# A Griffin-style decoder layer on one core: down-projection sums rescheduled over fourteen units, and the last half's embedding, squares and stores rearranged

## The chip, the cores and the metric

The kernel runs on one core of a Trainium2 chip. The metric is the device time of one execution in microseconds. TensorE (PE) multiplies matrices, VectorE (DVE), ScalarE (ACT) and GpSimd (POOL) work element by element, SyncE (SP) issues nearly all the transfers (DMA). Each engine runs its instructions in the order in which they stand in the program; an instruction that waits holds up everything behind it on its engine.

## The reference

One layer of a hybrid decoder, 1024 tokens by 1024 features, float32. What matters here comes after the two attention branches:

```
h  += SwiGLU(RMSNorm(h))                   # silu(n W_gate) * (n W_up), then W_down;  D_FF = 2816
h  += sigmoid(h W_g) * RMSNorm(p[i] W_p)   # a gated embedding of the layer
out = RMSNorm(h)
```

## The kernel before, in words

Every float32 product is made of three TensorE passes over operands split in a high and a low part (`split`, lines 130 to 132: a cast on ACT at L131, a subtraction on DVE at L132; `passes`, lines 134 to 139). Activations are held transposed, 128 features by 512 tokens to a tile; 512 tokens are a half.

**Gate and up, 985 to 1432 us.** The two wide products are made with a seven-product (Winograd) scheme. One unit `wino` is a block of 256 columns of one of the two weights: 7 products of 12 matmuls, some 19.4 us of TensorE. Even units u are gate units, odd ones up units; the loop `for n, u in enumerate(rest())` runs 19 units, n = 0 to 18, which are u = 3 to 21. The loop interleaves the products of neighbouring units. A product's weight block is split into a tile `wl` (three buffers) before TensorE may read it: cast on ACT, L132 on DVE. Two sums of weight blocks are made ahead on POOL (L969, L970) as soon as the unit's 1 MB of raw weights has landed, two more later (L986, L988). PSUM accumulators `pP`, `pQ`, `pR` are added to stored copies by DVE (`add`, L979). In an up unit the finished blocks are multiplied with those of the gate unit on POOL (L1034) or DVE (L1036), subtracted from each other on DVE (`sub`, L1027) and stored to `d_g`.

**Down sums.** The down projection uses the same scheme, so sums of blocks of its weight are made ahead, beside gate and up. `down_in(kk)` loads four blocks of 256 KB into half of the tile `spare` (L1113); `down_sums(kk, ...)` makes four sums in place on DVE (L1120, two operands in SBUF, 128x512) and stores each to `d_w` (L1121). There are KK = 11 such sets. Four loads of 512 KB (L1142) then fill `spare` with the first blocks for the down stage.

**Down, 1432 to 1650 us**, reads `d_g` and `d_w` back. **Gated embedding, 1650 us to the end:** three groups, (half 1, all 512 tokens), (half 0, first 256), (half 0, last 256). In each, for f = 0 to 7: load of the embedding tile e (L1231), scaling with gain and reciprocal root (L1232, DVE), 24 matmuls into `pg`, sigmoid (L1238, ACT), e = sg * e (L1239, DVE), h = e + h (L1241, DVE), square (L1245, ACT), and acc += square (L1246, DVE). Then the squares are summed over partitions by `rstd_cols` (matmuls `pm`, L168; `rstd_finish`, L172 on DVE and L173 on POOL), `spread` turns the result into a row broadcast over partitions (L742 on DVE, matmul `bc`, L745), and eight tiles are scaled (L1252, DVE) and stored (L1254, SP).

The program's order is made by a scheduler from its own model of the engines, so an edit in one place can move instructions elsewhere. `tc.issue_after(x)` keeps what stands under it behind instruction x.

Of the kernel before, what the change touches and what calls it, by code (L numbers as in the profile page):

```python
# [10 lines left out]
F32 = mybir.dt.float32  # L11
# [8 lines left out]
P = 128  # L20
# [31 lines left out]
def decoder_layer(ctx: ExitStack, tc: tile.TileContext, x, p, positions, g_mix, w_in, g_q_a, w_q_b,  # L52
# [104 lines left out]
    with ExitStack() as att:  # L157
# [341 lines left out]
        with ExitStack() as ml:  # L499
# [5 lines left out]
            def slot(tag, name, dtype=F32R):  # L505
                return qkp.tile([P, S], dtype, name=name, tag=tag, bufs=2 if tag == "vst" else 3)
# [450 lines left out]
    t1_factors(quarter[0], bc0)  # L957
    acc = out_group(1, 2, 2)

    FIRST = (1, 2, 5, 6, 7, 3, 4)  # L960
    firsts = iter((M, O, B))
    ORDER = (1, 5, 2, 6, 7, 3, 4)

    def wino(raw, order, ctile, ready):
# [11 lines left out]
            nc.scalar.copy(out=s[key], in_=pt)  # L976

        def add(key, pt):
            nc.vector.tensor_tensor(out=s[key], in0=pt, in1=s[key], op=ALU.add)  # L979
            return s[key]  # L980

        for n, i in enumerate(order):
# [141 lines left out]
    DIRECT = {1: (0, 0), 2: (0, 1), 4: (1, 1)}  # L1124
    before = None
    blocks = {}
    for n, u in enumerate(rest()):

        if 2 <= n < KK + 2:
            blocks[n - 2] = down_in(n - 2)  # L1130
        for _ in range(2):
            next(u)
        for _ in before or ():
            pass
        for _ in range(3):
            next(u)
        before = u
        if 3 <= n < KK + 3:
            down_sums(n - 3, blocks.pop(n - 3))
        if n == KK + 4:  # L1140
            for kk in range(0, 8, 2):
                nc.sync.dma_start(out=spare[:, kk:kk + 2, :], in_=wd[0, :, kk:kk + 2, hcol(0)])  # L1142

# [69 lines left out]
    for hf in (1, 0):  # L1213
        bc[hf] = spread(wk.tile([P, HALF], F32, name="diag", tag="rr", bufs=10), r_ple[:, 4 * hf:4 * hf + 4])
        if hf:
            es = wk.tile([P, HALF], F32, name="bcs", tag="bcs")
            nc.scalar.copy(out=es, in_=bc[hf])
            bc[hf] = es
    for hf, c0, n in ((1, 0, 4), (0, 0, 2), (0, 2, 2)):
        c = slice(c0 * P, (c0 + n) * P)  # L1220
        w_ = slice(0, n * P)
        s = slice(hf * HALF + c0 * P, hf * HALF + (c0 + n) * P)
        acc = wk.tile([P, 2, HALF], F32, name="acc", tag="rs", bufs=3)
        for f in range(NK):
            w = wpg[f // 2][:, f % 2]
            if hf == 1:
                raw = wk.tile([P, NK, P], F32, name="raw", tag="ls", bufs=3)
                nc.sync.dma_start(out=raw, in_=w_ple_gate[:, f * P:(f + 1) * P].rearrange("(k p) n -> p k n", p=P))
                split(w[:, 0], w[:, 1], raw)
            e = wk.tile([P, HALF], F32, name="e", tag="rr", bufs=10)[:, w_]  # L1230
            nc.sync.dma_start(out=e, in_=d_e[f * P:(f + 1) * P, s])  # L1231
            nc.vector.scalar_tensor_tensor(out=e, in0=e, scalar=gains[:, 1, f:f + 1], in1=bc[hf][:, c],  # L1232
                                           op0=ALU.mult, op1=ALU.mult)
            pg = ps.tile([P, HALF], F32, name="pg", **big())[:, w_]
            passes(pg, [((w[:, 0, k, :], w[:, 1, k, :]), (hsp[hf, k // 4][:, 0, k % 4, c], hsp[hf, k // 4][:, 1, k % 4, c]))
                        for k in range(NK)])
# [5 lines left out]
            if f == 0:  # L1242
                nc.scalar.activation(out=acc[:, 0, w_], in_=h, func=AF.Square, scale=1.0 / 32.0)
            else:
                nc.scalar.activation(out=sg, in_=h, func=AF.Square, scale=1.0 / 32.0)  # L1245
                nc.vector.tensor_tensor(out=acc[:, 0, w_], in0=acc[:, 0, w_], in1=sg, op=ALU.add)  # L1246
        r = wk.tile([P, 4], F32, name="r", tag="r", bufs=2)
        rstd_cols(acc[:, 0, :], r[:, 0:n], n)
        bo = spread(acc[:, 1, :], r[:, 0:n], n, B)[:, w_]
        for f in range(NK):  # L1250
            o = wk.tile([P, HALF], F32, name="o", tag="rr", bufs=10)[:, w_]
            nc.vector.scalar_tensor_tensor(out=o, in0=hres[:, f, s], scalar=gains[:, 2, f:f + 1], in1=bo,  # L1252
                                           op0=ALU.mult, op1=ALU.mult)
            nc.sync.dma_start(out=out[f * P:(f + 1) * P, s], in_=o)  # L1254
    dn.close()
    mo.close()

# [32 lines left out]
```

## Time and profile before

| | us |
|---|---|
| median of 3 runs (lowest, highest) | 1770.49 (1769.61, 1770.96) |
| the profiled execution | 1764.39 |
| its span, first to last instruction | 1762.7 |
| TensorE busy | 1689.8 (96%) |
| VectorE, ScalarE, GpSimd busy | 1159.9, 893.1, 368.1 |
| mean granted clock of TensorE, share of full | 0.987 |

The profiled execution is one single run, 6.1 us below the median of the others. Busy times of different engines overlap; idle time of an engine that nobody waits for costs nothing. The rows of the profile that matter stand below.

### The profile page before, as it was taken

To read this page: it belongs to the slowest core of one execution; us is meant where nothing else is said; L and a number is where in the kernel's file an instruction comes from. 1 tells how busy PE (TensorE), PEld (TensorE's weight loads), DVE (VectorE), ACT (ScalarE), POOL (GpSimd) and SP (SyncE) were. 2 spreads that over 40 slices of the span, in tenths; PEclk is the share of its full clock that TensorE was granted. 3 is DMA by queue.
4 is the path that set the end of the run, shared out by engine and by line. 5 is a ranking of instruction groups with operands and counts; after the bars stand their busy time and mean duration, and the time that the engine had idled before them with its cause. 6 is when DMAs were issued, how large, how long until landed. Compare 5 with 4: busy or idle time off the path is not lost.

```text
span 1762.7 us, 23332 instructions
## 1 busy us (share of the span) xinstructions
PE 1689.8 (96%) x8148; PEld 1406.3 (80%) x8148; DVE 1159.9 (66%) x2079; ACT 893.1 (51%) x1740; POOL 368.1 (21%) x393
## 2 busy tenths in 40 slices
PE   6999999999999999998999999899999999999995
PEld 5888878888787888886889778688888878888795
DVE  6667788768875877787368865744444545656655
ACT  5265676667775776676135533233333334445411
POOL 2011320000211433331001823344344310000000
PEclk9999999999999999999999899999999999999998
DMA  5211221213414321215763584842233338666422
GB/s 173 55 54 44 71 61 43 78 43 90 126 37 156 103 67 63 76 49 206 266 241 121 179 274 151 274 153 92 94 111 104 108 116 291 195 196 192 145 71 74
DMA packets 169400, 222.15 MB, mean 126 GB/s; under 512 B 23298, under 2 KB 100098, under 8 KB 169282
## 3 DMA queue, kind: packets, MB, share of 16 engines
q1 hardware_dynamic: 163250, 200.74, 35.4%
q0 software_dynamic: 6032, 19.93, 3.2%
q8 instruction: 64, 1.05, 0.3%
q14 instruction: 54, 0.44, 0.1%
HBM read 151.93 MB, written 67.90 MB: 125 GB/s over the span
## 4 chain that ended last, share of the span: by engine, by line
PE 72%; DVE 9%; issue 7%; DMA 7%; ACT 2%; POOL 2%; SPq 0%; POOLq 0%; DVEq 0%; ACTq 0%
PE pt L137 5%; PE pt L138 5%; PE pt L139 5%; PE pd L138 3%; PE pd L137 3%; PE pd L139 3%; PE pP L139 3%; PE pP L137 3%; PE pP L138 3%; DMA spare<-w_ffn_down 2%; PE pQ L137 2%; PE pQ L138 2%; PE pg L137 2%; PE pQ L139 2%; PE pg L139 2%
## 5 line engine op out<-in xcount | busy, mean ns | idle before, releaser
L137 PE MATMUL pt<-nTh,w_h 128*128 128x512 f32 (+1 forms) x480 | 190.8, 398 | 3.5 <-ACT go L355 2.4
L138 PE MATMUL pt<-nTl,w_h 128*128 128x512 f32 (+1 forms) x480 | 188.5, 393 | 0.0
L139 PE MATMUL pt<-nTh,w_l 128*128 128x512 f32 (+1 forms) x480 | 187.6, 392 | 0.0
L132 DVE TENSOR_TENSOR wl<-raw,wl 128x512 fp32r<-128x512 f32 x132 | 98.7, 750 | 97.5 <-ACT wl L131 97.0
L139 PE MATMUL pP<-b,wl 128*128 128x512 f32 x352 | 139.0, 397 | 11.4 <-DVE wl L132 11.4
L131 ACT CAST wl<-raw 128x512 fp32r<-128x512 f32 x132 | 82.0, 622 | 125.2 <-PE pP L139 53.4
L137 PE MATMUL pP<-b,wl 128*128 128x512 f32 x352 | 139.6, 397 | 5.7 <-ACT wl L131 3.5
L138 PE MATMUL pP<-b,wl 128*128 128x512 f32 x352 | 139.4, 396 | 0.0
L137 PEld LDWEIGHTS pt<-nTh,w_h 128*128 128x128 f32 (+1 forms) x480 | 89.7, 187 | 25.7 <-ACT go L355 5.9
L139 PEld LDWEIGHTS pt<-nTh,w_l 128*128 128x128 f32 (+1 forms) x480 | 89.8, 187 | 19.2
L138 PEld LDWEIGHTS pt<-nTl,w_h 128*128 128x128 f32 (+1 forms) x480 | 89.9, 187 | 18.2
L132 DVE TENSOR_TENSOR drs<-drr,drs 128x512 fp32r<-128x512 f32 x74 | 50.9, 690 | 76.3 <-ACT drs L131 76.3
L138 PE MATMUL pd<-drs,dls 128*128 128x512 f32 x296 | 100.7, 390 | 0.1
L139 PE MATMUL pd<-drs,dls 128*128 128x512 f32 x296 | 100.4, 389 | 0.0
L137 PE MATMUL pd<-drs,dls 128*128 128x512 f32 x296 | 99.9, 392 | 0.0
L131 ACT CAST drs<-drr 128x512 fp32r<-128x512 f32 x74 | 45.9, 623 | 103.2 <-PE pd L139 92.6
L139 PEld LDWEIGHTS pP<-b,wl 128*128 128x128 f32 x352 | 67.2, 191 | 29.8 <-DVE wl L132 15.9
L638 POOL TENSOR_SCALAR pw<-pw,st 128x128 f32<-128x128 f32 (+5 forms) x48 | 74.4, 1556 | 63.9 <-PE tp L652 13.9
L137 PEld LDWEIGHTS pP<-b,wl 128*128 128x128 f32 x352 | 67.4, 192 | 20.4 <-ACT wl L131 3.8
L138 PEld LDWEIGHTS pP<-b,wl 128*128 128x128 f32 x352 | 67.4, 191 | 14.2
L445 DVE TENSOR_TENSOR sz<-sz,T 128x512 f32<-128x512 f32 (+2 forms) x96 | 52.2, 550 | 33.8 <-PE T L443 33.0
L356 POOL DMA_DIRECT2D d_gate<-go x32 | 17.7, 554 | 260.2 <-ACT go L355 218.3
(371 smaller groups left out, 4792.6 us busy)
## 6 DMA issues: line engine op xcount, KB each, us to landing
d_g<-t SPq DMA_DIRECT2D x74, 256.0 KB, 2.0
drr<-d_g SPq DMA_DIRECT2D x74, 256.0 KB, 2.9
w_raw<-w_in SPq DMA_DIRECT2D x33, 512.0 KB, 4.4
raw<-w_ffn_gate SPq DMA_DIRECT2D x11, 1024.0 KB, 5.6
raw<-w_ffn_up SPq DMA_DIRECT2D x11, 1024.0 KB, 5.6
spare<-w_ffn_down SPq DMA_DIRECT2D x44, 256.0 KB, 3.8
d_w<-spare SPq DMA_DIRECT2D x44, 256.0 KB, 3.3
drr<-d_w SPq DMA_DIRECT2D x44, 256.0 KB, 2.7
```

The source lines that it names most:

```text
L131: nc.scalar.copy(out=h, in_=src)
L132: eng.tensor_tensor(out=l, in0=src, in1=r32(h), op=ALU.subtract)
L137: nc.tensor.matmul(ps, lhsT=ah, rhs=bh, start=first and i == 0, stop=False, **kw)
L138: nc.tensor.matmul(ps, lhsT=ah, rhs=bl, start=False, stop=False, **kw)
L139: nc.tensor.matmul(ps, lhsT=al, rhs=bh, start=False, stop=last and i == n - 1, **kw)
L356: nc.gpsimd.dma_start(out=dst, in_=go[0:rows, :])
L445: nc.vector.tensor_tensor(out=sz[:, c0:], in0=sz[:, c0:], in1=T[:, c0:], op=ALU.subtract)
L638: nc.gpsimd.tensor_scalar(out=pw[:, 0:nk], in0=pw[:, 0:nk], scalar1=st[:, 6:7], scalar2=None, op0=ALU.mult)
```

## The change

It has two parts. In gate and up, the eleven sets of down sums are spread: set kk is loaded at n = 2 + 5*kk//4 (2, 3, 4, 5, 7, 8, 9, 10, 12, 13, 14; before: 2 to 12) and summed one n later, and its sums are held behind the latest accumulator add of the unit, which is the one on `pP`. The last four loads of `spare` come one n later. In the gated embedding, half 0's embedding is loaded into one tile `en` (16 KB in each partition, four transfers of 512 KB) and scaled once over 512 tokens, in place of sixteen tiles of 256 tokens; the squares of the last f are not added to acc on DVE but summed by more matmuls into `pm`; the outputs are written over `hres`, and go out in four stores of two tiles, two of which ACT's queue issues in the last group.

```
@@ wino @@
         def add(key, pt):
-            nc.vector.tensor_tensor(out=s[key], in0=pt, in1=s[key], op=ALU.add)
+            latest["add"] = nc.vector.tensor_tensor(out=s[key], in0=pt, in1=s[key], op=ALU.add).ins
@@ loop over the units @@
+    when = {2 + 5 * kk // 4: kk for kk in range(KK)}
     for n, u in enumerate(rest()):
-        if 2 <= n < KK + 2:
-            blocks[n - 2] = down_in(n - 2)
+        if n in when:
+            blocks[when[n]] = down_in(when[n])
...
-        if 3 <= n < KK + 3:
-            down_sums(n - 3, blocks.pop(n - 3))
-        if n == KK + 4:
+        if n - 1 in when:
+            with tc.issue_after(latest["add"]):
+                down_sums(when[n - 1], blocks.pop(when[n - 1]))
+        if n == KK + 5:
@@ gated embedding @@
+        if hf == 0 and en is None:
+            en = slot(2, "en", [P, NK, HALF], F32)
+            for f in range(0, NK, 2):
+                nc.sync.dma_start(out=en[:, f:f + 2, :], in_=d_e[f * P:(f + 2) * P, hcol(0)]
+                                  .rearrange("(k p) n -> p k n", p=P))
+            for f in range(NK):
+                nc.vector.scalar_tensor_tensor(out=en[:, f, :], in0=en[:, f, :], scalar=gains[:, 1, f:f + 1], in1=bc[0],
+                                               op0=ALU.mult, op1=ALU.mult)
...
-            e = wk.tile([P, HALF], F32, name="e", tag="rr", bufs=10)[:, w_]
-            nc.sync.dma_start(out=e, in_=d_e[f * P:(f + 1) * P, s])
...
+            else:
+                e = en[:, f, c]
...
-                nc.vector.tensor_tensor(out=acc[:, 0, w_], in0=acc[:, 0, w_], in1=sg, op=ALU.add)
+                if f < NK - 1:
+                    nc.vector.tensor_tensor(out=acc[:, 0, w_], in0=acc[:, 0, w_], in1=sg, op=ALU.add)
-        rstd_cols(acc[:, 0, :], r[:, 0:n], n)
+        pt = ps.tile([P, HALF], F32, name="pm", **M)
+        for sq in (acc[:, 0, :], sg):
+            for i in range(n):
+                nc.tensor.matmul(pt[:, i:i + 1], lhsT=sq[:, i * P:(i + 1) * P], rhs=ones, start=sq is not sg and i == 0,
+                                 stop=sq is sg, skip_group_check=True)
+        rstd_finish(pt, r[:, 0:n], n)
...
-            nc.sync.dma_start(out=out[f * P:(f + 1) * P, s], in_=o)
+            if f % 2:
+                eng = nc.scalar if c0 and f % 4 == 1 else nc.sync
+                eng.dma_start(out=out[(f - 1) * P:(f + 1) * P, s].rearrange("(k p) n -> p k n", p=P),
+                              in_=hres[:, f - 1:f + 1, s])
```

The tile `en` takes the memory of `hs[1, 0]`, the first half of the features of half 1, so its loads wait for TensorE's last read of that. Lines behind the changed ones move by a few numbers: L979 becomes L980, L1027 L1028, L1034 L1035, L1036 L1037, L1120 and L1121 become L1121 and L1122; in the gated embedding L1232 becomes L1235 (half 0) and L1246 (half 1), L1239 L1255, L1241 L1257, L1246 L1263, L168 L1268, L1252 L1273, L1254 L1277.

How the order changes, at three places. The first is VectorE around the sums. In the program of before they stand between the splits (L132) and the adds (L979); this is where units u = 4 and 5 meet, 1100 to 1115 us:

```order
1328 L1120 TENSOR_TENSOR spare<-spare 128x512
1329 L979 TENSOR_TENSOR t<-pQ,t 128x512
1330 L132 TENSOR_TENSOR wl<-raw,wl 128x512 x2
1331 L1120 TENSOR_TENSOR spare<-spare 128x512
1332 L979 TENSOR_TENSOR t<-pR,t 128x512
1333 L132 TENSOR_TENSOR wl<-raw,wl 128x512
1334 L1120 TENSOR_TENSOR spare<-spare 128x512 x3
1335 L132 TENSOR_TENSOR wl<-s_10697,wl 128x512
```

In the changed program the first set stands behind the `pP` add of unit u = 6, and in each of the eleven units that carry one it stands thus:

```order
1325 L980 TENSOR_TENSOR t<-pP,t 128x512
1326 L1121 TENSOR_TENSOR spare<-spare 128x512
1327 L132 TENSOR_TENSOR wl<-raw,wl 128x512
1328 L1121 TENSOR_TENSOR spare<-spare 128x512 x3
1329 L132 TENSOR_TENSOR wl<-raw,wl 128x512
1330 L980 TENSOR_TENSOR t<-pQ,t 128x512
```

The sums have moved from all over the unit to one place behind the `pP` add, with one split between the first and the other three.

The second place is VectorE in the up unit u = 7, from its `pQ` add on, before:

```order
1370 L979 TENSOR_TENSOR t<-pQ,t 128x512
1371 L132 TENSOR_TENSOR wl<-raw,wl 128x512
1372 L1036 TENSOR_TENSOR t<-pP,t 128x512
1373 L1027 TENSOR_TENSOR t<-t 128x512
1374 L132 TENSOR_TENSOR wl<-raw,wl 128x512
1375 L1027 TENSOR_TENSOR t<-t 128x512 x2
1376 L979 TENSOR_TENSOR t<-pR,t 128x512
1377 L132 TENSOR_TENSOR wl<-raw,wl 128x512
```

and in the changed program:

```order
1341 L980 TENSOR_TENSOR t<-pQ,t 128x512
1342 L132 TENSOR_TENSOR wl<-raw,wl 128x512
1343 L1028 TENSOR_TENSOR t<-t 128x512
1344 L1037 TENSOR_TENSOR t<-pP,t 128x512
1345 L1028 TENSOR_TENSOR t<-t 128x512
1346 L132 TENSOR_TENSOR wl<-raw,wl 128x512
1347 L1028 TENSOR_TENSOR t<-t 128x512
1348 L980 TENSOR_TENSOR t<-pR,t 128x512
1349 L1028 TENSOR_TENSOR t<-t 128x512
1350 L132 TENSOR_TENSOR wl<-raw,wl 128x512
```

The first subtraction (now L1028) has moved ahead of the `pP` product, and one more now stands ahead of the last split shown; so it is in u = 7, 9, 11, 13 and 17. On POOL the third L1035 of these units now stands ahead of both sums of the next raw weights (L970, L971), where before it stood between the two.

The third place is the passage from group 1 to group 2 of the gated embedding, VectorE, before:

```order
1713 L1239 TENSOR_TENSOR e<-sg,e 128x512
1714 L1241 TENSOR_TENSOR hres<-e,hres 128x512
1715 L1246 TENSOR_TENSOR acc<-acc,sg 128x512
1716 L172 TENSOR_SCALAR r<-pm 128x4
1717 L742 TENSOR_SCALAR acc<-ident,r 128x128 x4
1718 L1252 SCALAR_TENSOR_TENSOR o<-hres,cols,bc 128x512 x8
1719 L1232 SCALAR_TENSOR_TENSOR e<-e,cols,bc 128x256 x2
```

and in the changed program, where L1255 and L1257 are the last f of group 1:

```order
1716 L1235 SCALAR_TENSOR_TENSOR en<-en,cols,bc 128x512 x2
1717 L1255 TENSOR_TENSOR e<-sg,e 128x512
1718 L1235 SCALAR_TENSOR_TENSOR en<-en,cols,bc 128x512 x2
1719 L1257 TENSOR_TENSOR hres<-e,hres 128x512
1720 L1235 SCALAR_TENSOR_TENSOR en<-en,cols,bc 128x512 x4
1721 L172 TENSOR_SCALAR r<-pm 128x4
1722 L742 TENSOR_SCALAR acc<-ident,r 128x128 x4
1723 L1273 SCALAR_TENSOR_TENSOR hres<-hres,cols,bc 128x512 x8
```

The eight scalings of `en` stand between and around the last product and sum of group 1, and ahead of L172; each waits for its transfer.

## Rows read from the trace of the kernel before

In a row of a timeline: start in us, duration, engine, line, operation, out<-in, count; in square brackets the engine's idle time ahead of it and what ended that.

**Rows 1.** The page, busy time of each engine with its share of the span and its count of instructions.

```profile
PE 1689.8 (96%) x8148; PEld 1406.3 (80%) x8148; DVE 1159.9 (66%) x2079; ACT 893.1 (51%) x1740; POOL 368.1 (21%) x393
```

**Rows 2.** TensorE's waits between 860 and 1460 us: who waited for whom, us in total, times, longest.

```profile
PE pP L139 <- DVE wl L132: 11.4, 10, 4.6
```

**Rows 3.** TensorE's timeline, the instructions that ended a wait in gate and up.

```profile
1008.13 0.50 PE L137 MATMUL pR<-b,wl 128*128 128x512 f32 x1 [0.59 <-DVE spare L979]
1017.12 0.50 PE L139 MATMUL pQ<-b,wl 128*128 128x512 f32 x1 [0.53 <-DVE wl L132]
1026.48 0.50 PE L139 MATMUL pP<-b,wl 128*128 128x512 f32 x1 [0.67 <-DVE wl L132]
1037.17 0.50 PE L137 MATMUL pP<-b,wl 128*128 128x512 f32 x1 [2.22 <-DVE spare L979]
1110.94 0.50 PE L139 MATMUL pP<-b,wl 128*128 128x512 f32 x1 [4.63 <-DVE wl L132]
1134.35 0.50 PE L139 MATMUL pP<-b,wl 128*128 128x512 f32 x1 [2.45 <-DVE wl L132]
1174.92 0.50 PE L139 MATMUL pP<-b,wl 128*128 128x512 f32 x1 [0.52 <-DVE wl L132]
1214.03 0.50 PE L139 MATMUL pP<-b,wl 128*128 128x512 f32 x1 [0.74 <-DVE wl L132]
```

**Rows 4.** The sums' line L1120: for what VectorE sat idle ahead of them, us and times.

```profile
  DMA spare<-w_ffn_down: 24.0, 10
```

**Rows 5.** VectorE's timeline between 1108 and 1134 us.

```profile
1108.99 0.69 DVE L1120 TENSOR_TENSOR spare<-spare 128x512 f32<-128x512 f32 x1 [5.15 <-DMA spare<-w_ffn_down]
1110.20 0.68 DVE L132 TENSOR_TENSOR wl<-raw,wl 128x512 fp32r<-128x512 f32 x1
1126.92 0.69 DVE L1027 TENSOR_TENSOR t<-t 128x512 f32<-128x512 f32 x1 [1.18 <-POOL t L1034]
1133.02 0.68 DVE L1120 TENSOR_TENSOR spare<-spare 128x512 f32<-128x512 f32 x1
```

**Rows 6.** Windows: from:to, length, then busy us and count of PE, its weight loads, DVE, ACT, POOL, the granted clock of TensorE as a share of full, DMA share, GB/s.

```profile
1037.00:1041.00 4.00, 3.83 (x17) 3.14 (x18) 2.01 (x4) 2.52 (x5) 0.00 (x0) 1.00 0.94 290
1111.00:1115.00 4.00, 4.00 (x11) 3.13 (x12) 3.93 (x4) 0.00 (x0) 2.71 (x2) 0.57 0.40 153
1135.00:1139.00 4.00, 4.00 (x12) 3.12 (x11) 2.79 (x3) 0.82 (x2) 1.04 (x1) 0.57 0.86 330
```

**Rows 7.** Timelines of VectorE, then GpSimd, around the end of the up unit u = 7, where the kernel before has no sums.

```profile
1164.24 0.69 DVE L132 TENSOR_TENSOR wl<-raw,wl 128x512 fp32r<-128x512 f32 x1 [2.51 <-ACT wl L131]
1169.97 1.77 DVE L1027 TENSOR_TENSOR t<-t 128x512 f32<-128x512 f32 x1 [0.73 <-POOL t L1034]
...
1167.39 1.29 POOL L969 TENSOR_TENSOR s<-raw 128x512 f32<-128x512 f32 x1 [1.02 <-DMA raw<-w_ffn_gate]
1169.89 1.29 POOL L970 TENSOR_TENSOR raw<-raw 128x512 f32<-128x512 f32 x1
```

**Rows 8.** TensorE's timeline in the last group of the gated embedding.

```profile
1737.95 0.38 PE L137 MATMUL pg<-hs,wpg 128*128 128x256 f32 x1 [1.24 <-ACT sg L1238]
1751.67 0.38 PE L168 MATMUL pm<-cols,acc 128*128 128x1 f32 x1 [7.72 <-DVE acc L1246]
```

**Rows 9.** Timelines of VectorE, then ScalarE, in the same stretch.

```profile
1739.71 0.48 DVE L1232 SCALAR_TENSOR_TENSOR e<-e,cols,bc 128x256 f32<-128x256 f32 x1 [2.54 <-DMA e<-d_e]
1749.14 0.42 DVE L1239 TENSOR_TENSOR e<-sg,e 128x256 f32<-128x256 f32 x1
1749.81 0.42 DVE L1241 TENSOR_TENSOR hres<-e,hres 128x256 f32<-128x256 f32 x1
1750.14 1.48 DVE L1246 TENSOR_TENSOR acc<-acc,sg 128x256 f32<-128x256 f32 x3
1755.56 3.22 DVE L1252 SCALAR_TENSOR_TENSOR o<-hres,cols,bc 128x256 f32<-128x256 f32 x8 [1.31 <-PE bc L745]
...
1738.72 0.38 ACT L1238 ACTIVATE sg<-pg 128x256 f32<-128x256 f32 x1
1750.32 0.42 ACT L1245 ACTIVATE sg<-hres 128x256 f32<-128x256 f32 x1 [0.59 <-DVE hres L1241]
```

**Rows 10.** SyncE's queue at the end (start, time over which it issued, count), then the list of transfers between 1655 and 1765 us: count, KB each, median us from issue to landing.

```profile
1756.07 3.77 SPq L1254 DMA_DIRECT2D out<-o  x8
...
out<-o SPq DMA_DIRECT2D x8, 256.0 KB, 3.1
out<-o SPq DMA_DIRECT2D x16, 128.0 KB, 1.8
```

**Rows 11.** The passage from group 1 to group 2: timelines of TensorE, then VectorE, then two lines of the list of transfers of the whole span.

```profile
1688.20 0.39 PE L137 MATMUL pg<-hs,wpg 128*128 128x512 f32 x1
1700.00 0.95 PE L168 MATMUL pm<-cols,acc 128*128 128x1 f32 x8
...
1690.37 0.74 DVE L1232 SCALAR_TENSOR_TENSOR e<-e,cols,bcs 128x512 f32<-128x512 f32 x1
1694.47 0.69 DVE L1239 TENSOR_TENSOR e<-sg,e 128x512 f32<-128x512 f32 x1 [2.57 <-ACT sg L1238]
...
raw<-w_ple_gate SPq DMA_DIRECT2D x8, 512.0 KB, 4.6
hres<-d_h SPq DMA_DIRECT2D x4, 1024.0 KB, 10.9
```

More of the change, by code (lines that the diff above doesn't have):

```diff
@@ L958, in decoder_layer @@
     acc = out_group(1, 2, 2)
+    latest = {}
     FIRST = (1, 2, 5, 6, 7, 3, 4)
@@ L1218, in decoder_layer @@
             bc[hf] = es
+    en = None
     for hf, c0, n in ((1, 0, 4), (0, 0, 2), (0, 2, 2)):
@@ L1229, in decoder_layer @@
                 split(w[:, 0], w[:, 1], raw)
-            e = wk.tile([P, HALF], F32, name="e", tag="rr", bufs=10)[:, w_]
-            nc.sync.dma_start(out=e, in_=d_e[f * P:(f + 1) * P, s])
-            nc.vector.scalar_tensor_tensor(out=e, in0=e, scalar=gains[:, 1, f:f + 1], in1=bc[hf][:, c],
-                                           op0=ALU.mult, op1=ALU.mult)
+            if hf:
+                e = wk.tile([P, HALF], F32, name="e", tag="rr", bufs=10)
+                nc.sync.dma_start(out=e, in_=d_e[f * P:(f + 1) * P, s])
+                nc.vector.scalar_tensor_tensor(out=e, in0=e, scalar=gains[:, 1, f:f + 1], in1=bc[hf],
+                                               op0=ALU.mult, op1=ALU.mult)
+            else:
+                e = en[:, f, c]
             pg = ps.tile([P, HALF], F32, name="pg", **big())[:, w_]
@@ L1245, in decoder_layer @@
                 nc.scalar.activation(out=sg, in_=h, func=AF.Square, scale=1.0 / 32.0)
-                nc.vector.tensor_tensor(out=acc[:, 0, w_], in0=acc[:, 0, w_], in1=sg, op=ALU.add)
+                if f < NK - 1:
+                    nc.vector.tensor_tensor(out=acc[:, 0, w_], in0=acc[:, 0, w_], in1=sg, op=ALU.add)
         r = wk.tile([P, 4], F32, name="r", tag="r", bufs=2)
-        rstd_cols(acc[:, 0, :], r[:, 0:n], n)
+        pt = ps.tile([P, HALF], F32, name="pm", **M)
[4 more added lines that the diff above has]
+        rstd_finish(pt, r[:, 0:n], n)
         bo = spread(acc[:, 1, :], r[:, 0:n], n, B)[:, w_]
         for f in range(NK):
-            o = wk.tile([P, HALF], F32, name="o", tag="rr", bufs=10)[:, w_]
-            nc.vector.scalar_tensor_tensor(out=o, in0=hres[:, f, s], scalar=gains[:, 2, f:f + 1], in1=bo,
+            nc.vector.scalar_tensor_tensor(out=hres[:, f, s], in0=hres[:, f, s], scalar=gains[:, 2, f:f + 1], in1=bo,
                                            op0=ALU.mult, op1=ALU.mult)
-            nc.sync.dma_start(out=out[f * P:(f + 1) * P, s], in_=o)
+            if f % 2:
+                eng = nc.scalar if c0 and f % 4 == 1 else nc.sync
+                eng.dma_start(out=out[(f - 1) * P:(f + 1) * P, s].rearrange("(k p) n -> p k n", p=P),
+                              in_=hres[:, f - 1:f + 1, s])
     dn.close()
```

## The prediction, made before the changed kernel ran

> **What bounds the kernel now.** I began with the page: TensorE is busy for 96% of the span [rows 1], so a gain can only come out of the rest, from its waits and its clock. The list of its waits says where they lie. In gate and up nearly all go by one name, the low part of a split weight block that VectorE delivers: 11.4 us in ten waits [rows 2]. TensorE's timeline then separates large from ordinary ones: 4.63 us at 1110.94 and 2.45 us at 1134.35 stand out, and there is one of 2.22 us at 1037.17 for an add; later, when no down sum is left, one wait recurs in each pair of units, as the 0.52 and 0.74 us shown [rows 3]. So half a microsecond is the price of a pair as such, and what exceeds it needs a cause.
>
> The cause is in VectorE's timeline. At 1108.99 a down sum starts after 5.15 us of idleness for its weights; the split that TensorE wants starts at 1110.20, right behind [rows 5], and TensorE goes on at 1110.94. Nothing kept that split but its place in the queue. In all VectorE sat idle for 24.0 us, ten times, in front of these sums until a transfer had landed [rows 4]. The other large wait has another mixture: at 1126.92 VectorE waits 1.18 us for GpSimd's product, and then a down sum (1133.02) stands just ahead of the split [rows 5].
>
> The windows behind the two large waits show a second price: the granted clock is 0.57 in four microseconds, that is, most of them at the lower of the two levels, 1.2 GHz; behind the wait of 2.22 us it stayed at 1.00 [rows 6]. Four microseconds at 0.57 lose 4 x 0.43 = 1.7 us each.
>
> In the tail TensorE waits 1.24 us, then 7.72 us between its last `pg` product and the sum of squares [rows 8]. Before the 7.72 us VectorE had to wait for embedding tiles (2.54 us at 1739.71); afterwards it was busy with a pile of small operations whose last are three additions of squares [rows 9]. The end of the stage is therefore VectorE's.
>
> **Part one: the down sums.** No instruction is removed, and TensorE's order in gate and up is the same. The eleven sets start at unit 6, so units before that lose them; and a set is summed one unit (some 20 us) after its loads are issued. A unit is long against the 4 to 5 us that transfers of this kind take, so I cost the 24.0 us of idleness at nothing from now on. What this removes on TensorE: all of 4.63; 2.45 down to 0.5; 2.22 down to about 0.3, since the add remains; 0.67 and 0.53; 0.59 down to about 0.3. That is 4.63 + 1.95 + 1.9 + 0.67 + 0.53 + 0.3 = 10.0 us. With both large waits the clock should stay up: 2 x 1.7 = 3.4 us more. Gross gain 13.4.
>
> What it adds: the units from 6 to 18 now carry 4 sums each in eleven of them, 4 x 0.6 = 2.4 us of VectorE (0.69 each, starts 0.6 apart). They stand behind the `pP` add. There the timeline of unit 7 has an idle 2.51 us, ahead of the split at 1164.24 [rows 7], so the sums fit nearly exactly, and the cover is thin. The more doubtful matter is how these up units end. Subtractions move ahead of `pP`'s product and of the last split, and GpSimd's third product moves ahead of its sums of raw weights. For this the trace gives two bounds. Lower: it saves GpSimd's product the 1.02 us for raw weights and VectorE the 0.73 us for that product [rows 7], which would do away with a usual wait of some 0.5 us: -0.5 a unit. Upper: in unit 5 the same order of subtractions cost the 2.45 us of 1134.35, 1.9 above the usual, and there a down sum stood ahead of the split too, which is no longer so. Unit 5 had its sums late and directly at the split; unit 7 with sums behind `pP` resembles the undisturbed one, so I take +0.2 for each of the five (7, 9, 11, 13, 17): +1.0. From -2.5 to +9.5, and both ends stay in the range.
>
> One row bears on this. At 1169.97 a VectorE subtraction took 1.77 us where its like takes 0.69, and it ended only after GpSimd's sum at 1169.89 was well under way [rows 7]. The Trainium skill ("SBUF — State Buffer", section "Who interferes with whom") says that a VectorE instruction with two inputs in SBUF and a GpSimd instruction that reads SBUF exclude each other for the whole instruction, and that whoever came first holds the port. The trace agrees: 1.77 is 0.69 and about one more microsecond. By that rule the twenty sums of those five units each meet GpSimd's products with some chance; if one a unit is hit, five times 1.1 = 5.4 us more of VectorE, of which only what passes the idle 2.51 us reaches TensorE.
>
> Transfers keep their number and size. SyncE's queue gets the stores of the sums behind the sums, one unit later than loads; a raw load behind them may land later by about one sum, 0.7 us, which GpSimd's wait of 1.02 us shows to be near the edge. That too is inside the +1.0.
>
> **Part two: the passage from group 1 to group 2.** The loads of `en` can start when TensorE has read half of the last product of group 1: 1688.20 plus twelve matmuls of 0.23 = 1690.9. A transfer of 512 KB takes 4.6 us in this stage [rows 11], so the first lands near 1695.5. For those behind it I estimate the distance from the 330 GB/s that a DMA share of 0.86 moved [rows 6]: 384 at full share, 524 KB in 1.4 us, so they land near 1696.9, 1698.3 and 1699.7. VectorE's order then gives: two scalings of 0.74 us [rows 11] until 1697.0, the last product of group 1 (1694.47 before) until 1697.7, two scalings until 1699.2, the last sum until 1699.9, and with ACT's square, some 0.6, the `pm` matmuls have their data near 1700.5. TensorE was at this place at 1700.00 [rows 11]; the new first block of `pm` and two more products bring it there at about 1701.1. L172 follows behind the other four scalings, near 1702.6, and was at 1701 before; `bc` stands 38 products behind and covers that. The slack is half a microsecond; I take 0. The other end: if the loads go like `hres`, 10.9 us to a megabyte [rows 11], which is 21.8 for the two of `en`, the last lands near 1712; but those were issued among the down stage's loads, and `en`'s are alone, so for the bound I go part of the way and let TensorE wait 3 to 5 us.
>
> **Part three: the tail.** The 1.24 us should vanish: a sigmoid was late for it, and sigmoids write to tiles of a ring of ten (tag `rr`) that the embedding and the outputs used too and now leave; sixteen scalings of 0.48 us also become eight, done earlier. Two extra blocks of `pm` matmuls stand in the way, of groups 1 and 2: 0.8 and 0.4 us by the 0.95 for eight [rows 11]. These cancel, so the last `pg` still ends near 1751.67 - 7.72 = 1743.95, or at 1743.9. From there one chain: sigmoid 0.38, product 0.42, sum 0.42, square 0.42 [rows 9] and four hand-overs of at most 0.09 (the square of 1750.32 against 1749.81 + 0.42), I take 0.05: 1.85 us in place of 7.72. The saved addition leaves, and the same number of `pm` matmuls follows. That makes -5.9. From `pm` to the first scaled output it was 1755.56 - 1751.67 = 3.9 us, at the lower clock; the wait ahead being shorter, I give it 0.5 less for a clock that has not fallen so long: -0.5 (0 to -0.8). Stores: before, eight at 0.5 us to an issue, the last issued at 1755.56 + 3.9 and landed 1.8 later [rows 10], 5.7 in all. Now the last leaves when the eighth output is done, 3.22 [rows 9], and 256 KB takes 1.8 to 3.1: between 5.0 and 6.3, I take 5.4: -0.3. Tail -6.7, between -8 and -5.
>
> **Sum.** -13.4 + 1.0 - 6.7 = -19.1 us. The profiled execution took 1764.39: 1745.3. It lies 6.1 us below the median of the three runs, and nothing in the trace says why, so I carry the difference over: 1770.5 - 19.1 = 1751.4.
>
> **The rivals.**
> *The new order is the bound.* In five up units VectorE has four more operations, some of them at 1.77 in place of 0.69 us beside GpSimd [rows 7], and the wait at the last split grows to the 2.45 us of unit 5 each time. Behind the wait of that size the clock fell [rows 6], so each costs 1.9 + 1.7 = 3.6 us above the usual. Five make +18, the gain of the other places 20.1: about 1768.5 against the median; if the gate units (6, 8, 12, 14, 16, 18) with a shifted split wait one microsecond too, 1774.5, slower. For it: unit 5 has that order, and it waited. Against it: the sum ahead of its split, and 2.51 us of idleness at the new place.
> *Waits only move.* The large waits go, but the sums' queue place gives back half; the tail gains alone in full: -13.4/2 - 6.7 = -13, 1757.5. With nothing from part one, 1763.8.
> *`en` is late.* Passage +3 to +5, tail -6.7: 1755.5.
> *More than I take.* Order in the up units saves its half microsecond, and hidden waits go: 1747.
>
> **Chances.** Forecast, within 4 us of 1751.4: 0.50. Better than that: 0.10. Waits move by half: 0.16. `en` late: 0.10. Tail alone, about 1764: 0.05. New order the bound, near 1768.5: 0.04, and slower 0.05. A measurement of this kernel can tell about 0.2%, 3.5 us, from no change. Faster by more than that 0.92, within it 0.03, slower 0.05. The range from 1744 to 1761 holds the first four and leaves the last out.
>
> **What would show it.** In the profile after: VectorE idle in front of the sums for transfers near zero; no wait above 1 us on TensorE between 1000 and 1430 us; granted clock 1.0 from 1000 to 1740; in the tail one wait of about 2 us in place of 7.72, and the first scaled output about 6 us after the last `pg`. I am wrong if waits near 2.5 us, with clock dips behind them, stand at the last splits of units 7 to 17; if TensorE waits for `pm` near 1701; or if the end is set by ACT's two stores.

## The result, and the profile after

The changed kernel takes 1753.88 us (median of 4 runs, 1752.99 to 1755.31), the kernel before 1770.3 (4 runs beside it): a ratio of 0.9908, 95% interval 0.9891 to 0.9925, that is 16.4 us less. 1751.4 was forecast, the range was 1744 to 1761.

The profiled execution of the changed kernel took 1753.11 us, its span is 1751.2. Against [rows 1] the page shows TensorE hardly changed, and transfers that take longer from issue to landing; for the two shown the page of before has 5.6 and 3.3 us:

```profile
PE 1688.5 (96%) x8164; PEld 1407.9 (80%) x8164; DVE 1162.4 (66%) x2068; ACT 893.5 (51%) x1740; POOL 368.0 (21%) x393
...
raw<-w_ffn_gate SPq DMA_DIRECT2D x11, 1024.0 KB, 6.2
...
d_w<-spare SPq DMA_DIRECT2D x44, 256.0 KB, 6.3
```

To compare the traces I cut them at four instructions of TensorE. The first two are the first product behind the start of gate and up, and the first product of the down stage; TensorE's timeline of before and then of after:

```profile
991.25 0.80 PE L137 MATMUL pP<-b,wl 128*128 128x512 f32 x1 [3.50 <-ACT wl L131]
1432.59 0.50 PE L137 MATMUL pd<-dwl 128*128 128x512 f32 x1 [0.71 <-ACT dwl L131]
```

```profile
997.02 0.80 PE L137 MATMUL pP<-b,wl 128*128 128x512 f32 x1 [4.19 <-ACT wl L131]
1428.32 0.50 PE L137 MATMUL pd<-dwl 128*128 128x512 f32 x1 [0.71 <-ACT dwl L131]
```

The other two cuts are the first and the end of the last `pg` product (before 1650.02 and 1743.95, after 1645.94 and 1739.74).

| stretch, us | before | after | difference |
|---|---|---|---|
| to the first product of gate and up | 991.25 | 997.02 | +5.8 |
| gate and up | 441.3 | 431.3 | -10.0 |
| down | 217.4 | 217.6 | +0.2 |
| gated embedding to the end of the last `pg` | 93.9 | 93.8 | -0.1 |
| from there to the end | 18.7 | 11.4 | -7.3 |

Everything that was changed gained 17.3 us. The first stretch is the same code in both kernels and took 5.8 us more in this execution; so the spans differ by 11.5 us only, and the medians by 16.4.

TensorE's waits between 860 and 1460 us, to be read beside [rows 2]:

```profile
PE pP L139 <- DVE wl L132: 9.3, 8, 1.9
PE pP L137 <- ACT wl L131: 4.2, 1, 4.2
PE pP L137 <- DVE t L980: 0.5, 1, 0.5
```

The same name leads as before, but its longest wait is 1.9 us and no longer 4.6. TensorE's timeline shows where seven of the eight stand (the other, at 1087.70, took 0.48), beside [rows 3]:

```profile
1126.97 0.50 PE L139 MATMUL pP<-b,wl 128*128 128x512 f32 x1 [0.89 <-DVE wl L132]
1166.80 0.50 PE L139 MATMUL pP<-b,wl 128*128 128x512 f32 x1 [1.46 <-DVE wl L132]
1206.52 0.50 PE L139 MATMUL pP<-b,wl 128*128 128x512 f32 x1 [1.34 <-DVE wl L132]
1246.77 0.50 PE L139 MATMUL pP<-b,wl 128*128 128x512 f32 x1 [1.88 <-DVE wl L132]
1286.49 0.50 PE L139 MATMUL pP<-b,wl 128*128 128x512 f32 x1 [1.35 <-DVE wl L132]
1325.44 0.50 PE L139 MATMUL pP<-b,wl 128*128 128x512 f32 x1 [0.57 <-DVE wl L132]
1365.18 0.50 PE L139 MATMUL pP<-b,wl 128*128 128x512 f32 x1 [1.37 <-DVE wl L132]
```

The rows at 1166.80, 1206.52, 1246.77, 1286.49 and 1365.18 are the ends of the up units 7, 9, 11, 13 and 17, which now carry sums: 1.48 us in the mean. Unit 15, at 1325.44, carries none: 0.57. Before, all six were at 0.40 to 0.74.

The clock between 1005 and 1425 us, before and then after (columns as in [rows 6]):

```profile
1005.00:1425.00 420.00, 405.30 (x1757) 330.52 (x1756) 222.58 (x301) 146.84 (x254) 155.35 (x110) 0.99 0.44 147
```

```profile
1005.00:1425.00 420.00, 410.13 (x1800) 336.65 (x1799) 235.69 (x310) 151.15 (x261) 162.95 (x112) 1.00 0.46 152
```

The dips of [rows 6] are gone, the mean is 1.00. TensorE runs its matmuls of gate and up in the same order in both kernels, so its time can be compared matmul by matmul. Waits aside, the matmuls between the wait of 1110.94 and that of 1134.35 took 1.75 us less than before, and those from there to the end of unit 7 took 1.68 less. That is the price of the two dips.

In the tail TensorE's timeline, beside [rows 8]:

```profile
1740.21 0.60 PE L1268 MATMUL pm<-cols,acc 128*128 128x1 f32 x4 [0.47 <-ACT sg L1254]
1741.64 0.61 PE L1268 MATMUL pm<-cols,sg 128*128 128x1 f32 x4 [0.82 <-ACT sg L1261]
```

The second block of `pm` starts 1.9 us behind the end of the last `pg`, where 7.72 us stood.

### The profile page after: what moved, and what is told of

It reads as the page before. It is cut to its first block, busy times and chain, and to the rows that moved or that the text cites. A ratio compares the mean times of both kernels' runs of the same rounds, so it can differ in the third digit from the quotient of the medians.

```text
span 1751.2 us, 23280 instructions
## 1 busy us (share of the span) xinstructions
PE 1688.5 (96%) x8164; PEld 1407.9 (80%) x8164; DVE 1162.4 (66%) x2068; ACT 893.5 (51%) x1740; POOL 368.0 (21%) x393
## 4 chain that ended last, share of the span: by engine, by line
PE 78%; issue 7%; DVE 7%; DMA 4%; ACT 3%; POOL 2%; SPq 0%; DVEq 0%; POOLq 0%; ACTq 0%
PE pt L137 5%; PE pt L138 5%; PE pt L139 5%; PE pP L139 4%; PE pP L137 4%; PE pP L138 4%; PE pd L138 3%; PE pd L137 3%; PE pd L139 3%; PE pg L137 2%; PE pg L138 2%; PE pb L137 2%; PE pg L139 2%; PE pb L138 2%; PE pb L139 2%
## 5 line engine op out<-in xcount | busy, mean ns | idle before, releaser
L132 DVE TENSOR_TENSOR wl<-raw,wl 128x512 fp32r<-128x512 f32 x132 | 110.3, 837 | 102.2 <-ACT wl L131 101.6
L139 PE MATMUL pP<-b,wl 128*128 128x512 f32 x352 | 137.3, 392 | 9.3 <-DVE wl L132 9.3
L137 PE MATMUL pP<-b,wl 128*128 128x512 f32 x352 | 138.1, 392 | 4.7 <-ACT wl L131 4.2
L138 PE MATMUL pP<-b,wl 128*128 128x512 f32 x352 | 137.7, 391 | 0.0
L132 DVE TENSOR_TENSOR drs<-drr,drs 128x512 fp32r<-128x512 f32 x74 | 50.9, 690 | 76.3 <-ACT drs L131 76.3
L638 POOL TENSOR_SCALAR pw<-pw,st 128x128 f32<-128x128 f32 (+5 forms) x48 | 74.3, 1554 | 65.5 <-PE tp L652 13.8
L138 PEld LDWEIGHTS pP<-b,wl 128*128 128x128 f32 x352 | 66.6, 189 | 13.8
```

The source lines that it names most:

```text
L132: eng.tensor_tensor(out=l, in0=src, in1=r32(h), op=ALU.subtract)
L137: nc.tensor.matmul(ps, lhsT=ah, rhs=bh, start=first and i == 0, stop=False, **kw)
L138: nc.tensor.matmul(ps, lhsT=ah, rhs=bl, start=False, stop=False, **kw)
L139: nc.tensor.matmul(ps, lhsT=al, rhs=bh, start=False, stop=last and i == n - 1, **kw)
L638: nc.gpsimd.tensor_scalar(out=pw[:, 0:nk], in0=pw[:, 0:nk], scalar1=st[:, 6:7], scalar2=None, op0=ALU.mult)
```

## The experiments

Kernels that are compared ran on the same chip. Runs of one and the same kernel still differ by 1 to 13 us (the kernel before from 1764.1 to 1771.7 in 20 runs, the sums alone from 1754.3 to 1767.6 in 10), so medians and intervals decide between kernels, and the trace's stretches, which repeat to about a microsecond in gate and up (430.7 to 431.9 in six traces with the sums moved), say where the time went.

**The two parts apart.** The changed kernel with the old embedding stage, that is, of the diff only the first, and the old kernel with the new stage, only the second:

```
...
+    when = {2 + 5 * kk // 4: kk for kk in range(KK)}
...
+            with tc.issue_after(latest["add"]):
...
```

```
...
+            en = slot(2, "en", [P, NK, HALF], F32)
...
+        for sq in (acc[:, 0, :], sg):
...
+                eng = nc.scalar if c0 and f % 4 == 1 else nc.sync
...
```

> The changed kernel with the gated embedding of the kernel before: only the down sums are moved. My theory (the two parts are independent and add up; by the two traces gate and up gained 10.0 us and the tail 7.3): about 1760.3 us, 10 us faster than before, TensorE's waits between 985 and 1432 us as in the changed kernel (eight on the low part of a split, 9.3 us together, none over 2), the 7.7 us wait for the squares back. Rival (the moved sums gain little by themselves, the tail most): 1765 us or more.

> The kernel before with the gated embedding of the changed one: only the tail. My theory: 7.3 us faster than before, about 1763 us, the waits of 4.6 and 2.5 us in gate and up and the clock dips behind them still there; no wait of TensorE over 1 us between 1645 us and the last product of the last group. Rival (the tail's gain hung on gate and up as well, by transfers that are spread otherwise): less than 4 us.

Measured, against 1768.82 of before beside them: the sums alone 1758.99 us, ratio 0.9950 (0.9933 to 0.9968); the tail alone 1760.42, ratio 0.9958 (0.9940 to 0.9975). In the traces gate and up take 431.1 us with the sums moved and 441.1 without, and the stretch behind the last `pg` 18.2 without the new tail and 12.6 with it. With the tail alone the waits are those of before; in TensorE's list:

```profile
PE pP L139 <- DVE wl L132: 10.5, 10, 4.9
PE pP L137 <- DVE spare L979: 2.4, 1, 2.4
```

The parts add up within the noise: 9.8 and 8.4 us by the medians, 18.2 together where both at once brought 16.4; 10.2 and 6.1 by the stretches (the tail of after itself: 7.3). The rivals fall. One expectation held by half: with the tail alone the clock fell behind the wait of 4.9 us, but behind the other large one, 2.28 us here, it stayed at 1.00 (1140 to 1144 us). So the fall behind a wait of that size does not come in every execution.

**Without the hold-back.**

```
-            with tc.issue_after(latest["add"]):
-                down_sums(when[n - 1], blocks.pop(when[n - 1]))
+            down_sums(when[n - 1], blocks.pop(when[n - 1]))
```

> The changed kernel without the hold-back of the sums behind the add: the loads are still spread over fourteen units, but the sums stand where the scheduler puts them. My theory (the place of the sums in VectorE's queue makes the wait, not the rate of the loads): the idle time of VectorE ahead of the sums for transfers comes back, waits of TensorE of 2 us and more with it, most of gate and up's 10 us is lost, about 1761 to 1763 us. Rival (fewer sets to a unit and later loads suffice): like the changed kernel, 1754 us.

Measured 1760.72 us, ratio 0.9960 (0.9946 to 0.9975). Gate and up take 439.7 us. The sums' idle time ahead of them, and then two rows of TensorE's timeline:

```profile
  DMA spare<-w_ffn_down: 22.4, 9
```

```profile
1111.53 0.50 PE L139 MATMUL pP<-b,wl 128*128 128x512 f32 x1 [3.69 <-DVE wl L132]
1135.24 0.50 PE L139 MATMUL pP<-b,wl 128*128 128x512 f32 x1 [2.77 <-DVE wl L132]
```

The scheduler pulls the sums to the front again (they stand between 996 and 1147 us, before between 994 and 1146), though the loop names later units, and with them nearly all of the loss returns. The list of units by itself gains 1.6 of the 10 us; the hold-back is what the first part lives on. In the changed kernel the sums' line has no such idle time at all.

**The order of the subtractions.** What makes the 1.5 us at the end of an up unit with sums? VectorE's timeline there, unit 7 of the changed kernel, then GpSimd's:

```profile
1152.53 1.78 DVE L132 TENSOR_TENSOR wl<-raw,wl 128x512 fp32r<-128x512 f32 x1
1154.24 2.13 DVE L1121 TENSOR_TENSOR spare<-spare 128x512 f32<-128x512 f32 x3
1156.28 0.68 DVE L132 TENSOR_TENSOR wl<-raw,wl 128x512 fp32r<-128x512 f32 x1
1160.14 0.69 DVE L1028 TENSOR_TENSOR t<-t 128x512 f32<-128x512 f32 x1 [1.19 <-POOL t L1035]
1162.56 1.78 DVE L132 TENSOR_TENSOR wl<-raw,wl 128x512 fp32r<-128x512 f32 x1
1165.47 0.68 DVE L1028 TENSOR_TENSOR t<-t 128x512 f32<-128x512 f32 x1
1166.07 0.68 DVE L132 TENSOR_TENSOR wl<-raw,wl 128x512 fp32r<-128x512 f32 x1
```

```profile
1152.10 1.66 POOL L1035 TENSOR_TENSOR t<-t 128x512 f32<-128x512 f32 x1 [5.14 <-DVE t L980]
1157.11 1.29 POOL L989 TENSOR_TENSOR raw<-raw 128x512 f32<-128x512 f32 x1 [3.35 <-DVE wl L132]
1158.36 1.74 POOL L1035 TENSOR_TENSOR t<-t 128x512 f32<-128x512 f32 x1
1160.80 1.29 POOL L970 TENSOR_TENSOR s<-raw 128x512 f32<-128x512 f32 x1 [0.70 <-DMA raw<-w_ffn_gate]
1162.17 1.62 POOL L971 TENSOR_TENSOR raw<-raw 128x512 f32<-128x512 f32 x1
```

The last row of VectorE is the split for which TensorE waits until 1166.80; a subtraction stands just ahead of it, and the first subtraction, the row at 1160.14, has waited for GpSimd's product (the row at 1158.36) with VectorE's own product of `pP` behind it. The down sums have a part in this: GpSimd's sum at 1157.11, which stands ahead of its product, waited 3.35 us for the split behind the down sums, where the same sum in unit 15, which has none, waited 2.20. In the next kernel the subtractions are queued behind that product, which restores VectorE's order of before; the sums stay, and GpSimd's order stays that of the changed kernel.

```
-                nc.vector.tensor_tensor(out=g, in0=pt, in1=g, op=ALU.mult)
+                last = nc.vector.tensor_tensor(out=g, in0=pt, in1=g, op=ALU.mult).ins
...
-            if 7 not in done and (1, 1) in done and (0, 1) in done:
-                sub(7, t_tile(), done[1, 1], done[0, 1])
+            if 7 not in done and (1, 0) in done:
+                with tc.issue_after(last):
+                    sub(7, t_tile(), done[1, 1], done[0, 1])
```

> The changed kernel with the subtractions of an up unit held behind VectorE's product of the last accumulator, which gives VectorE in units 7, 9, 11, 13 and 17 its order of before, sums otherwise in place. My theory (the waits of 1.3 to 1.9 us at the ends of these units, 0.9 above the usual, come from the order of the subtractions, since one more stands ahead of the split and the product waits behind one that waits for GpSimd): waits back to about 0.5, 5 x 0.9 = 4.5 us faster than the changed kernel, about 1749.5 us. Rival 1 (the four sums themselves push the splits): waits stay at 1.3 to 1.9, 1754 us. Rival 2 (raw weights land later, 6.4 in place of 5.5 us): waits stay or grow, since GpSimd's sums of raw weights stand ahead of its product again, 1754 to 1757 us.

Measured 1748.35 us, ratio 0.9895 (0.9874 to 0.9916); gate and up 426.8 us against 431.3; the mean wait at the ends of the five units 0.69. To rule out the chip it ran again beside the changed kernel, with a third variant that has the sums in gate units only (there the last four loads of `spare` come two turns of the loop later still):

```
...
-    when = {2 + 5 * kk // 4: kk for kk in range(KK)}
+    when = {2: (0, 1), 4: (2, 3), 6: (4, 5), 8: (6,), 10: (7,), 12: (8,), 14: (9,), 16: (10,)}
...
```

> The changed kernel once more, beside the two variants below on the same chip. All theories: about 1754 us, 0.991 of before; gate and up 431 us from the first product behind the start to the first down product, the tail (last gate product to the end) 11.4 to 12.6 us.

> The subtractions behind the product once more. My theory: 4 to 5 us below the changed kernel of the same call. Rival (the 5.5 us seen between two calls were the chips): within 2 us of it.

> The changed kernel with the sums in gate units alone: two sets each in units 6, 8 and 10, one each in 12, 14, 16, 18 and 20; the up units then have their order of before without anything held back. If the order of the subtractions costs the 0.9 us a unit: waits at the ends of units 7 to 17 back to about 0.5, and the gate units, which have no subtractions, take eight sums (4.8 us) or four without a wait over 0.5: 4.5 us below the changed kernel, like the variant with subtractions held back. Rival (VectorE's time is what counts, wherever the sums stand): new waits of 1 us and more in the gate units 6, 8 and 10, and no gain beyond 2 us.

Measured, against 1767.84 of before:

| | median us | ratio (95%) | gate and up, us | mean wait, ends of units 7, 9, 11, 13, 17 |
|---|---|---|---|---|
| changed kernel | 1751.67 | 0.9902 (0.9885 to 0.9920) | 431.9 | 1.54 |
| subtractions held back | 1748.69 | 0.9887 (0.9871 to 0.9904) | 426.9 | 0.82 |
| sums in gate units | 1747.34 | 0.9880 (0.9867 to 0.9894) | 425.9 | 0.42 |

Two rows of TensorE's timeline with the subtractions held back (second execution), then two with the sums in gate units, the ends of units 7 and 11:

```profile
1167.14 0.50 PE L139 MATMUL pP<-b,wl 128*128 128x512 f32 x1 [0.90 <-DVE wl L132]
1245.53 0.50 PE L139 MATMUL pP<-b,wl 128*128 128x512 f32 x1 [0.74 <-DVE wl L132]
```

```profile
1165.62 0.50 PE L139 MATMUL pP<-b,wl 128*128 128x512 f32 x1 [0.40 <-DVE wl L132]
1243.16 0.50 PE L139 MATMUL pP<-b,wl 128*128 128x512 f32 x1 [0.43 <-DVE wl L132]
```

So VectorE's order at the end of the unit is 0.7 of the 1.1 us by which a unit with sums exceeds one that has none near (1.54, 0.82 and 0.42); 0.4 remains when the order is that of before. My expectation of waits back to about 0.5 was therefore too good. By the medians the gain was 3.0 us where I expected 4 to 5, and 4.3 where I expected 4.5. The intervals of the times overlap, between the changed kernel and the second by much, so the times alone prove little; gate and up in the traces, 5.0 and 6.0 us shorter, goes the same way. Eight sums in a gate unit cost no wait over 0.5 us there: the rival falls.

GpSimd's order and the raw weights, which land later than before (6.2 in place of 5.6 us), are not what made the 0.7 us. GpSimd in unit 7 with the subtractions held back:

```profile
1159.26 1.74 POOL L1035 TENSOR_TENSOR t<-t 128x512 f32<-128x512 f32 x1
1161.62 1.29 POOL L970 TENSOR_TENSOR s<-raw 128x512 f32<-128x512 f32 x1 [0.62 <-DMA raw<-w_ffn_gate]
```

Its product still stands ahead of its sums of raw weights, which still land 6.2 us after their issue, and yet TensorE's wait shrank. What the remaining 0.4 us is stays open: with the sums in gate units the up units lose the sums' time on VectorE, GpSimd has its order of before again, and the gate weights land sooner (5.4 us), all at once.

**The tail's three edits, each alone** (with the sums moved). The embedding in one tile; the last squares on TensorE; outputs in place with paired stores:

```
...
+                e = en[:, f, c]
...
```

```
...
+                if f < NK - 1:
+                    nc.vector.tensor_tensor(out=acc[:, 0, w_], in0=acc[:, 0, w_], in1=sg, op=ALU.add)
...
+        for sq in (acc[:, 0, :], sg):
...
```

```
...
+            nc.vector.scalar_tensor_tensor(out=hres[:, f, s], in0=hres[:, f, s], scalar=gains[:, 2, f:f + 1], in1=bo,
...
+                eng = nc.scalar if c0 and f % 4 == 1 else nc.sync
...
```

> Of the tail's three edits the one tile for the last half's embedding alone, with the sums moved: squares all added on VectorE, outputs in tiles of their own and eight stores. My theory (the embedding's late tiles made VectorE's pile): the tail from the last gate product to the end falls from 18.2 us to about 13, the wait for the squares from 7.7 to about 2.7 us. Rival (the ring of ten tiles, taken by outputs, made the embedding late, so what counts is that outputs leave the ring): 16 us or more.

> Of the tail's three edits the sum of the last squares on TensorE alone, with the sums of the down weights moved. My theory (the embedding was all): the tail from the last gate product to the end stays near 18 us, at most 0.4 (one addition) below the 18.2 of the kernel without any tail edit; the three groups lose up to 1.3 us to the two extra blocks of matmuls. Rival (the last addition was in the chain that ended last): 17.5 us or less.

> Of the tail's three edits the outputs in place and in paired stores alone, with the sums of the down weights moved. My theory: outputs leave the ring of ten tiles and SyncE's queue loses stores, so some embedding tiles may come earlier, but sixteen scalings on VectorE stay: tail 15 to 18 us in place of 18.2; the last output lands as long after the first scaled tile as before (6.8 to 7.1 us to the end). Rival (the stores bound the end): 1 us or more less from the first scaled tile to the end.

TensorE's wait ahead of the `pm` block that ended the last group, from the lists of waits, in the order none, embedding, squares, stores:

```profile
PE pm L168 <- DVE acc L1249: 7.5, 1, 7.5
```

```profile
PE pm L168 <- DVE acc L1262: 2.4, 1, 2.4
```

```profile
PE pm L1256 <- DVE acc L1251: 5.8, 1, 5.8
```

```profile
PE pm L168 <- DVE acc L1250: 4.4, 1, 4.4
```

| us | none | embedding | squares | stores | all |
|---|---|---|---|---|---|
| gated embedding to the last `pg` | 93.9 | 92.5 | 93.8 | 92.5 | 93.8 |
| from there to the end | 18.2 | 12.4 | 17.3 | 14.6 | 11.4 |
| together | 112.1 | 104.9 | 111.1 | 107.0 | 105.2 |

These are one trace each; the stretch behind the last `pg` was 11.4 to 12.6 us in eight traces with all three edits. The tile for the embedding brings 7.2 us alone, as much as all three (6.9), so no gain of the others beside it can be seen. But the stores alone bring 5.1 too, and a stretch of 14.6 where I had expected 15 to 18: my theory was too narrow there. The edits are substitutes more than parts of a sum. Outputs written in place leave the ring of ten tiles and halve the stores ahead of the embedding's loads; either may be what made the embedding late, which these runs don't separate.

From the first scaled tile to the end it takes 6.6 to 7.9 us in the five traces with eight stores and 6.3 to 7.1 in the nine with four: the number of stores changes the end by little. The squares on TensorE put 1.3 us of `pm` matmuls into the groups, as expected, and end the stretch at 17.3, 0.9 below the 18.2. That is the side of the rival (17.5 or less), not mine (17.8 or more), by one trace. With the embedding late, VectorE's last addition was in the chain that ended last; why the gain is twice such an addition (0.42) stays open.

**Without the sums.**

```
...
-            nc.vector.tensor_tensor(out=a[dst], in0=a[x], in1=a[y], op=op)
             nc.sync.dma_start(out=d_w[LEFT[i], kk], in_=a[dst])
...
```

> The changed kernel without VectorE's 44 down sums; their loads and stores stay (what is stored are the plain blocks). A floor for gate and up: if the sums cost only by what they do to the up units' order, the waits of units 7 to 17 are 0.4 to 0.9 and gate and up takes about 425.5 us, as in the two variants with the order of before; if VectorE's time for sums costs beside that, 2 us or more below them.

This failed as a floor, and in a way that teaches something. Its one execution took 1765.22 us, gate and up 446.4. TensorE, then GpSimd, then SyncE's queue, then what that queue waited for between 1055 and 1105 us:

```profile
1103.12 0.80 PE L139 MATMUL pP<-b,wl 128*128 128x512 f32 x1 [13.82 <-DVE wl L132]
```

```profile
1095.69 1.26 POOL L970 TENSOR_TENSOR s<-raw 128x512 f32<-128x512 f32 x1 [14.41 <-DMA raw<-w_ffn_gate]
```

```profile
1087.68 0.33 SPq L1121 DMA_DIRECT2D d_w<-spare  x1
1088.11 0.38 SPq L841 DMA_DIRECT2D raw<-w_ffn_gate  x1
```

```profile
SPq L1114 <- DMA d_w<-spare: 14.8, 10, 5.3
SPq L1121 <- DMA spare<-w_ffn_down: 14.2, 11, 4.0
```

Without the sums nothing on VectorE holds the stores back. Loads of `spare` and stores to `d_w` then alternate in SyncE's queue, the loads waiting for stores and the stores for loads, and a load of raw weights is issued at 1088.11, behind them. GpSimd waits 14.4 us for it, TensorE 13.8. So the sums also pace SyncE's queue. Without the hold-back, but with the sums in place, the longest wait of TensorE for a split was 3.7 us. What the sums cost in all stays open.

**The version that the runs point to**: sums in gate units, and of the tail the embedding alone.

> The version that the runs point to: the sums in gate units alone, and of the tail's edits only the one tile for the embedding. Gate and up 426 us, the three groups and the tail 104.9 us (105.8 with all three edits): about 1 us below the variant with sums in gate units, 1746.5 us, 0.9875 of before. Rival (the extra matmuls and the paired stores pay for themselves): 1747.5 or more.

Measured 1746.99 us (1744.83 to 1751.52, 6 runs), ratio 0.9897 (0.9874 to 0.9919) against 1766.15 of before. It is faster than the kernel before; against the variant with all three tail edits (0.9880) no gain can be told, so the expected microsecond was not found. Gate and up took 425.6 us and the embedding's groups 92.5, but the stretch behind the last `pg` 14.1 in this trace, where the end came 4.0 us after the last store was issued, against 2.7 in the other trace with the embedding alone. Groups and tail together are 106.6 us here and 104.9 there, so the 7.2 us of the embedding alone are 5.5 in this second trace; with all three edits it is 105.2 to 106.4.

## Why the prediction was right, point by point

The forecast was -19.1 us; the medians say -16.4, the changed stretches of the traces -17.3.

*The removed waits*, -10.0 forecast: the six rows of [rows 3] that I took away sum to 11.1 us. At those six matmuls only 0.89 is left, -10.2; a new wait of 0.52 us, at another matmul (1054.26), makes it -9.7. Idleness ahead of the sums for transfers, costed at nothing, is nothing. Right.

*The clock*, -3.4: no stretch at the lower clock between 1005 and 1425 us, and 1.75 + 1.68 = 3.4 us less behind the two large waits. Right. In the kernel without the hold-back the waits of 3.69 and 2.77 us came back, and behind them the granted clock was 0.72 from 1111 to 1117 us and 0.66 from 1135 to 1140.

*The five up units with sums*, +0.2 each, +1.0: this is the term that I mis-sized. The waits went from 0.55 to 1.48 us, +0.9 each, +4.7, inside the bounds of -2.5 to +9.5. With it failed one of the signs that I had set down, no wait above 1 us: there are five, of 1.34 to 1.88. I reasoned that unit 7 with sums would resemble the undisturbed unit 7, since 2.51 us of idleness take them in. They do take them in, all but a microsecond: the split behind them starts 4.95 us after the `pP` add (1151.33 to 1156.28), where unit 15 without sums has 3.86. But I counted VectorE's operations, not their order: 0.7 us of it is their order, the subtraction ahead of the split and the product queued behind a subtraction that waits for GpSimd together, as the held-back variant shows, and unit 5 of the kernel before, with the same order, had been a warning that I put down to its late sum. The overlap with GpSimd is there as the row led me to expect: in unit 7 the splits at 1152.53 and 1162.56 take 1.78 us each beside GpSimd's rows. Here the trace agrees with the Trainium skill ("SBUF — State Buffer", section "Who interferes with whom"), by which a VectorE instruction with two inputs in SBUF and a GpSimd instruction that reads SBUF contend. None of the waits reached the 2.45 us of the rival, and no dip of the clock followed. The raw weights land 0.6 us later, as I took it (0.7).

*Sum of gate and up*: -12.4 forecast, -10.0 found. The waits listed fell by 4.8 us and the two dips give 3.4. The other 1.8 us lie nearly all in the first 46 us, up to the matmul of 1037.17, where I had forecast nothing beside the waits; 0.5 of them in the first 17 us, where the clock is low at first in both kernels (granted 0.84 in the first 14 us before, 0.88 after). For the rest I have no cause. That this gain and the mis-sized term partly cancel is luck.

*The passage*, 0 with half a microsecond of slack: VectorE and TensorE there, after.

```profile
1691.34 1.40 DVE L1235 SCALAR_TENSOR_TENSOR en<-en,cols,bc 128x512 f32<-128x512 f32 x2 [3.50 <-DMA en<-d_e]
1694.58 0.69 DVE L1257 TENSOR_TENSOR hres<-e,hres 128x512 f32<-128x512 f32 x1
```

```profile
1697.06 0.95 PE L1268 MATMUL pm<-cols,sg 128*128 128x1 f32 x8
```

The embedding stage begins 4.1 us earlier here (1645.94 against 1650.02), so 4.1 is to be taken from my times: first scaling 1691.4 forecast and 1691.34 found, the last sum's end 1695.8 and 1695.27, TensorE at the block of `sg` 1697.0 and 1697.06. The data were there at 1696.0, 1.1 us ahead; no wait. For L172 my terms add up to 1702.9, not 1702.6; nothing hung on it.

*The tail*, -6.7: -7.3 in this trace, -6.1 with the tail alone. The chain of 1.85 us measured 1.90. From the last `pg` to the first scaled tile I gave 5.25, it is 4.86 (4.9 to 5.8 in the eight traces): from `pm` on it was 0.9 us shorter, not 0.5, with the granted clock at 1.00 there where it had been 0.50. From the first scaled tile to the end I counted 5.7 us before and 5.4 after; the traces have 7.1 and 6.6. I had read both too short by more than a microsecond, and only their difference came out (-0.3 forecast, -0.5 found). That the 1.24 us of [rows 8] and the extra `pm` blocks cancel held (93.9 and 93.8); the blocks measured 1.3 us, where I had put 1.2 and the row that I went by gives 1.4. What the sum did not tell is the share of the edits: the embedding alone does as much as all three, and the stores alone most of it.

*Carrying over the 6.1 us* by which the profiled execution lay below the median: right, since the medians differ by 16.4 us and the two profiled executions by 11.3. Why that one execution was the faster no run shows; the last section has one thing that varies between executions.

Of the rivals, "waits only move" came nearest in its mechanism: of the gross 13.4 us of gate and up a quarter, 3.4, is missing (the half that it assumed makes 1757.1 by its own terms, not 1757.5). "`en` is late" did not happen, though its 1755.5 is nearer to the measured time.

## What to carry to other kernels

Work that fills an engine's idle time has to be held at its place in the queue: moved to later units but left to the scheduler it drifted back to the front, ahead of what TensorE waited for. When it fits the idle time, look at what it does to the order of what stands behind it, since there two thirds of what an up unit still lost lay. And of several edits at one end, try each alone: here one of three did as much as all three, and a second most of it.

## What the runs showed of the hardware that I had not expected

The first 991 us, the same code in both kernels, took 5.8 us longer in the profiled execution of after. Part of it is the granted clock: one window there, before and then after.

```profile
245.00:250.00 5.00, 5.00 (x24) 4.16 (x24) 4.64 (x9) 4.95 (x12) 3.39 (x5) 1.00 0.45 104
```

```profile
245.00:250.00 5.00, 5.00 (x21) 4.13 (x21) 4.64 (x11) 4.95 (x11) 4.04 (x6) 0.66 0.47 124
```

At 245 us TensorE is busy all the time in both, and the last wait ahead of that is the same (0.37 us, at 242.7 and 243.4), and yet the clock is 0.66 in one and 1.00 in the other. Five microseconds at 0.66 lose 1.7 us. So executions of the same code differ by microseconds through the clock, and a change of a few tenths of a per cent is read from the stretches that it touches, not from two spans. The rest of the 5.8 us I did not follow up.
